# Runs of 60 KiB instead of 64 KiB in a streaming loss kernel, and three last chunks instead of two

## The chip, the cores and the metric

The kernel runs on one core of a Trainium2 chip; the other cores are idle. The metric is the device time of one execution in microseconds (us).

HBM is the chip's main memory and SBUF the core's own. 16 DMA engines move data between the two in packets; in the big transfers of this kernel one packet is the run of one partition (7680 packets of 64 KiB for 60 transfers of 128 partitions). VectorE and ScalarE compute; GpSimd issues most of the DMAs, which stand in its queue until the engines take them.

## The reference, cut to what matters

```python
pred   : (8192, 8192) float32 in 0.01 .. 0.99
target : (8192, 8192) float32, 0 or 1
pred = clip(pred, 1e-7, 1 - 1e-7)
out  = -(target * log(pred) + (1 - target) * log(1 - pred))
```

As the target is 0 or 1, the result is -log|pred + target - 1|. Three arrays of 268.44 MB cross the memory interface: two in, one out. Nothing is reused.

## The kernel before

The data is seen as 128 partitions by 524288 columns, cut into chunks. A chunk is one contiguous region of HBM, and each partition takes one contiguous run of it, so the row pitch in HBM equals the run: 16384 columns of float32 are 64 KiB. Two rings in SBUF (buffers that are filled round and round) hold two chunks: the pred in float32, overwritten in place by the result, and the target, which the DMA casts to bfloat16.

```python
RING = 32768
BIG = 16384

def plan(total):
    head = [(8192, [4096, 4096]), (8192, [8192])]
    tail = [(8192, [4096, 4096]), (8192, [4096, 2048, 2048])]
    n = (total - sum(w for w, _ in head + tail)) // BIG
    chunks = head + [(BIG, [BIG // 2] * 2)] * n + tail
    ...
def dram(flat, k):
    part = flat[cols[k] * P : (cols[k] + widths[k]) * P]
    return part.rearrange("(p w) -> p w", p=P)

def load(k):
    queue = nc.sync if k == 0 else nc.gpsimd
    nc.gpsimd.dma_start(out=span(ring_t, ...), in_=dram(target_f, k))
    queue.dma_start(out=span(ring_p, ...), in_=dram(pred_f, k))

def front(col, w):     # VectorE: clip; pred + (target - 1).  ScalarE: Abs, Ln
    ...
def back(col, w):      # VectorE: times -1
    ...
# ... (cut) per chunk: front of both pieces, back of both, store, then the loads that fit;
# in the last two chunks each piece is stored on the sync queue as soon as it is ready
```

## Time and profile before

| what | before |
|---|---|
| time, median of 3 runs | 1866.57 us (1865.54 to 1866.64) |
| span of the profiled run | 1864.5 us |
| VectorE, ScalarE busy | 60%, 48% |
| DMA row | full in all 40 slices |
| read and written in HBM | 536.87 MB, 268.44 MB |
| common packet of 64 KiB | 2418 ns |

The DMA row tells how much of the time the 16 engines had a packet in hand. It doesn't tell whether a packet was slow; for that one needs the packet durations, which are in the trace's records. A chain of waits, in contrast, has to go through something at every moment; here it goes through compute and "issue" for most of the span (ScalarE 24%, VectorE 15%, issue 25%), although the transfers beside them have no gap.

### The profile page before, as it was taken

The page shows a single profiled execution, that of the slowest core. Times are in us where ns is not written, and L with a number is a line of the kernel's source. Part 1 is how long each engine was busy: PE and PEld are TensorE (multiplying, and loading weights), DVE is VectorE, ACT ScalarE, POOL GpSimd, SP SyncE. Part 2 cuts the span into 40 slices and gives each one's busy share as a digit, 9 for nine tenths or more (in the row PEclk, how much of TensorE's full clock was granted, in tenths as well). Part 3 has the DMA queues.
Part 4 walks back from the last instruction along what each step waited for, and adds up shares of the span by engine and source line. Part 5 has one row for each costly group of instructions (what it writes and reads, how often), then busy time and mean ns, then how long its engine had stood idle before and what let it go on. Part 6 is the DMA issues. An engine that isn't in the chain of part 4 may idle for free.

```text
span 1864.5 us, 601 instructions
## 1 busy us (share of the span) xinstructions
DVE 1121.4 (60%) x205; ACT 899.3 (48%) x138; POOL 58.4 (3%) x103
## 2 busy tenths in 40 slices
DVE  4557654576545765557655576655766556665576
ACT  3366433664346643366433664335653356533566
POOL 1000000000000000000000000000000000000000
DMA  9999999999999999999999999999999999999999
GB/s 303 358 352 337 351 399 370 340 349 344 396 372 349 340 345 401 378 339 350 344 390 378 356 339 340 396 388 340 342 352 380 389 356 339 340 385 393 347 337 394
DMA packets 15124, 671.13 MB, mean 360 GB/s; under 512 B 1680, under 2 KB 1680, under 8 KB 1680
## 3 DMA queue, kind: packets, MB, share of 16 engines
q0 software_dynamic: 14256, 658.51, 98.5%
q1 hardware_dynamic: 864, 12.58, 1.6%
q14 instruction: 4, 0.03, 0.0%
HBM read 536.87 MB, written 268.44 MB: 432 GB/s over the span
## 4 chain that ended last, share of the span: by engine, by line
DMA 33%; issue 25%; ACT 24%; DVE 15%; POOL 1%; POOLq 0%; DVEq 0%; PEldq 0%
DMA ring_p<-in_pred_dram 31%; ACT ring_p L93 12%; ACT ring_p L92 12%; DVE ring_p L89 8%; DVE ring_p L86 4%; DVE ring_p L97 4%; DMA out_dram<-ring_p 1%; DMA ring_t<-in_target_dram 1%; POOL out_dram L80 1%; POOL ring_t L75 0%; POOLq L80 0%; DVEq L89 0%; PEldq L166 0%; POOLq L76 0%; POOLq L75 0%
## 5 line engine op out<-in xcount | busy, mean ns | idle before, releaser
L92 ACT ACTIVATE ring_p<-ring_p 128x8192 f32<-128x8192 f32 (+2 forms) x68 | 450.2, 6621 | 950.1 <-DVE ring_p L89 950.1
L89 DVE SCALAR_TENSOR_TENSOR ring_p<-ring_t,ring_p 128x8192 f32<-128x8192 bf16 (+2 forms) x68 | 556.9, 8190 | 2.5 <-DMA ring_t<-in_target_dram 0.2
L86 DVE TENSOR_SCALAR ring_p<-ring_p 128x8192 f32<-128x8192 f32 (+2 forms) x68 | 283.7, 4172 | 384.7 <-DMA ring_p<-in_pred_dram 384.7
L97 DVE TENSOR_SCALAR ring_p<-ring_p 128x8192 f32<-128x8192 f32 (+2 forms) x68 | 283.9, 4176 | 344.3 <-ACT ring_p L93 344.3
L93 ACT ACTIVATE ring_p<-ring_p 128x8192 f32<-128x8192 f32 (+2 forms) x68 | 450.7, 6628 | 2.2
L80 POOL DMA_DIRECT2D out_dram<-ring_p x32 | 22.3, 696 | 842.7 <-DVE ring_p L97 842.7
L76 POOL DMA_DIRECT2D ring_p<-in_pred_dram x33 | 17.7, 535 | 912.6 <-DMA out_dram<-ring_p 912.6
L75 POOL DMA_DIRECT2D ring_t<-in_target_dram x34 | 18.7, 551 | 0.8 <-PEq L166 0.8
L127 ACT ACT_TABLE_LOAD x1 | 1.3, 1283 | 0.7 <-PEq L155 0.7
L126 DVE MEMSET warm<- 1x8 f32 x1 | 0.1, 65 | 0.8 <-PEq L155 0.8
L127 ACT ACTIVATE warm<-warm 1x8 f32<-1x8 f32 x1 | 0.2, 208 | 0.0
L155 POOL MEMSET const-float32-0.0<- 128x1 f32 x1 | 0.1, 98 | 0.2 <-issue 0.2
L155 POOL MEMSET const-bfloat16-1.0<- 128x1 bf16 x1 | 0.1, 101 | 0.0
L155 POOL MEMSET const-uint8-127<- 128x1 uint8 x1 | 0.1, 99 | 0.0
L155 POOL MEMSET const-float32-1.0<- 128x1 f32 x1 | 0.1, 98 | 0.0
## 6 DMA issues: line engine op xcount, KB each, us to landing
ring_t<-in_target_dram POOLq DMA_DIRECT2D x30, 4096.0 KB, 50.0
ring_p<-in_pred_dram POOLq DMA_DIRECT2D x3, 4096.0 KB, 37.4
ring_t<-in_target_dram POOLq DMA_DIRECT2D x4, 2048.0 KB, 29.4
out_dram<-ring_p POOLq DMA_DIRECT2D x2, 4096.0 KB, 35.9
out_dram<-ring_p SPq DMA_DIRECT2D x3, 2048.0 KB, 16.2
ring_p<-in_pred_dram SPq DMA_DIRECT2D x1, 4096.0 KB, 19.7
out_dram<-ring_p SPq DMA_DIRECT2D x2, 1024.0 KB, 10.7
ring_p<-in_pred_dram POOLq DMA_DIRECT2D x30, 38.4
```

Of the source, the lines that this page charges most:

```text
L75: nc.gpsimd.dma_start(out=span(ring_t, cols[k], widths[k]), in_=dram(target_f, k))
L76: queue.dma_start(out=span(ring_p, cols[k], widths[k]), in_=dram(pred_f, k))
L80: queue.dma_start(out=dram(out_f, k)[:, off : off + w], in_=span(ring_p, cols[k] + off, w))
L86: nc.vector.tensor_scalar(out=p, in0=p, scalar1=EPS, scalar2=1 - EPS, op0=Alu.max, op1=Alu.min)
L89: nc.vector.scalar_tensor_tensor(out=p, in0=t, scalar=1.0, in1=p, op0=Alu.subtract, op1=Alu.add)
L92: nc.scalar.activation(out=p, in_=p, func=Act.Abs)
L93: nc.scalar.activation(out=p, in_=p, func=Act.Ln)
L97: nc.vector.tensor_scalar(out=p, in0=p, scalar1=-1.0, scalar2=None, op0=Alu.mult)
L126: nc.vector.memset(warm, 1.0)
L127: nc.scalar.activation(out=warm, in_=warm, func=Act.Ln)
L155: nc = _bacc.Bacc("TRN2", target_bir_lowering=False, num_devices=1)
```

## The change

Its intent: rows in HBM that lie an odd number of 4 KiB apart (15 x 4 KiB) rather than a power of two, in case such rows collide; and loads of the whole end ahead of the last big store. 15360 goes 34 times into 524288 and leaves 2048, so the end has three chunks (7680, 7680 and 2048 columns) in place of two. Its core:

```diff
-RING = 32768
-BIG = 16384
+BIG = 15 * 1024
+HALF = BIG // 2
@@ plan
-    tail = [(8192, [4096, 4096]), (8192, [4096, 2048, 2048])]
-    chunks = head + [(BIG, [BIG // 2] * 2)] * n + tail
+    spots = [(HALF, 0), (HALF, HALF)]
+    spots += [(BIG, k % 2 * BIG) for k in range(1, n - 1)]
+    end = (n - 1) % 2 * BIG
+    return spots + [(HALF, end), (HALF, end + HALF), (last, 2 * BIG)]
@@ the order is now written out ... (cut)
+        for k in range(2, n - 3):
+            front(k, (0, 2)); front(k, (1, 2)); back(k, (0, 2)); back(k, (1, 2))
+            if k < n - 4:
+                store(k)
+                for j in range(k + 2, n if k == n - 5 else k + 3):
+                    load(j)
+        store(n - 4)
+        a, b, c = n - 3, n - 2, n - 1
+        front(a)
+        front(b, (0, 2))
+        front(b, (1, 2))
+        back(a)
+        store(a)
+        front(c)
+        back(b)
+        store(b)
+        back(c)
+        store(c)
```

The last chunks are stored in pieces: two of 7680 columns and one of 2048, where there were three of 4096 and two of 2048. (The first two chunks are now computed whole.)

More of the change, by code (lines that the diff above doesn't have):

```diff
@@ L8 @@
 EPS = 1e-7
-RING = 32768
-BIG = 16384
+BIG = 15 * 1024
+HALF = BIG // 2
 def plan(total):
-    head = [(8192, [4096, 4096]), (8192, [8192])]
-    tail = [(8192, [4096, 4096]), (8192, [4096, 2048, 2048])]
-    n = (total - sum(w for w, _ in head + tail)) // BIG
-    chunks = head + [(BIG, [BIG // 2] * 2)] * n + tail
-    assert sum(w for w, _ in chunks) == total
-    return chunks, len(chunks) - len(tail)
+    n, last = divmod(total, BIG)
+    assert n > 4 and 0 < last <= 2048
+    spots = [(HALF, 0), (HALF, HALF)]
+    spots += [(BIG, k % 2 * BIG) for k in range(1, n - 1)]
+    end = (n - 1) % 2 * BIG
+    return spots + [(HALF, end), (HALF, end + HALF), (last, 2 * BIG)]
 @with_exitstack
@@ L49, with chunk, spot, store @@
     R, C = pred.shape
-    pred_f = pred.rearrange("r c -> (r c)")
-    target_f = target.rearrange("r c -> (r c)")
-    out_f = out.rearrange("r c -> (r c)")
-    total = R * C // P
+    spots = plan(R * C // P)
+    n = len(spots)
+    widths = [w for w, _ in spots]
+    cols = [sum(widths[:k]) for k in range(n)]
+    def chunk(ap, k):
+        flat = ap.rearrange("r c -> (r c)")
+        return flat[cols[k] * P : (cols[k] + widths[k]) * P].rearrange("(p w) -> p w", p=P)
     pool = ctx.enter_context(tc.tile_pool(name="rings", bufs=1))
-    ring_p = pool.tile([P, RING], fp32, name="ring_p", tag="ring_p")
-    ring_t = pool.tile([P, RING], bf16, name="ring_t", tag="ring_t")
+    ring = [P, 2 * BIG + widths[-1]]
+    ring_p = pool.tile(ring, fp32, name="ring_p", tag="ring_p")
+    ring_t = pool.tile(ring, bf16, name="ring_t", tag="ring_t")
     warm = pool.tile([1, 8], fp32, name="warm", tag="warm")
-    chunks, tail = plan(total)
-    widths = [w for w, _ in chunks]
-    cols = [sum(widths[:k]) for k in range(len(chunks))]
-    def dram(flat, k):
-        part = flat[cols[k] * P : (cols[k] + widths[k]) * P]
-        return part.rearrange("(p w) -> p w", p=P)
-    def span(ring, col, w):
-        c = col % RING
-        assert c + w <= RING
-        return ring[:, c : c + w]
+    def spot(ring, k, part=(0, 1)):
+        w, c = spots[k]
+        i, m = part
+        return ring[:, c + i * w // m : c + (i + 1) * w // m]
     def load(k):
         queue = nc.sync if k == 0 else nc.gpsimd
-        nc.gpsimd.dma_start(out=span(ring_t, cols[k], widths[k]), in_=dram(target_f, k))
-        queue.dma_start(out=span(ring_p, cols[k], widths[k]), in_=dram(pred_f, k))
-    def store(k, off, w):
-        queue = nc.sync if k >= tail else nc.gpsimd
-        queue.dma_start(
-            out=dram(out_f, k)[:, off : off + w], in_=span(ring_p, cols[k] + off, w)
-        )
-    def front(col, w):
-        p, t = span(ring_p, col, w), span(ring_t, col, w)
+        nc.gpsimd.dma_start(out=spot(ring_t, k), in_=chunk(target, k))
+        queue.dma_start(out=spot(ring_p, k), in_=chunk(pred, k))
+    def store(k):
+        queue = nc.sync if k >= n - 3 else nc.gpsimd
+        queue.dma_start(out=chunk(out, k), in_=spot(ring_p, k))
+    def front(k, *part):
+        p, t = spot(ring_p, k, *part), spot(ring_t, k, *part)
         nc.vector.tensor_scalar(
@@ L93, in front, with back @@
         nc.scalar.activation(out=p, in_=p, func=Act.Ln)
-    def back(col, w):
-        p = span(ring_p, col, w)
+    def back(k, *part):
+        p = spot(ring_p, k, *part)
         nc.vector.tensor_scalar(out=p, in0=p, scalar1=-1.0, scalar2=None, op0=Alu.mult)
-    stored = loaded = 0
-    def load_what_fits():
-        nonlocal loaded
-        while (
-            loaded < len(chunks) and cols[loaded] + widths[loaded] <= stored + RING
-        ):
-            load(loaded)
-            loaded += 1
-    waiting = []
-    def finish_one():
-        nonlocal stored
-        k, off, w = waiting.pop(0)
-        back(cols[k] + off, w)
-        if k >= tail:
-            store(k, off, w)
-        elif off + w == widths[k]:
-            store(k, 0, widths[k])
-        else:
-            return
-        stored = cols[k] + off + w
-        load_what_fits()
     with tc.manual_schedule():
-        load_what_fits()
+        for k in range(3):
+            load(k)
         nc.vector.memset(warm, 1.0)
         nc.scalar.activation(out=warm, in_=warm, func=Act.Ln)
-        for k, (_, pieces) in enumerate(chunks):
-            off = 0
-            for w in pieces:
-                front(cols[k] + off, w)
-                waiting.append((k, off, w))
-                off += w
-                if len(waiting) > 1:
-                    finish_one()
-            while waiting and k < tail:
-                finish_one()
-        while waiting:
-            finish_one()
+        front(0)
+        front(1)
+        back(0)
+        store(0)
+        back(1)
+        store(1)
+        load(3)
+        for k in range(2, n - 3):
+            front(k, (0, 2))
+            front(k, (1, 2))
+            back(k, (0, 2))
+            back(k, (1, 2))
+            if k < n - 4:
[14 more added lines that the diff above has]
+        store(c)
 _INS = ['pred', 'target']
```

## The prediction

> **What bounds the kernel now.** I read the page of the profile first, then its waits, then the stretches of time, then the timeline of one chunk, and last the DMA packet records of the trace. The page says who is busy:
>
> ```profile
> DVE 1121.4 (60%) x205; ACT 899.3 (48%) x138; POOL 58.4 (3%) x103
> ...
> DMA  9999999999999999999999999999999999999999
> ...
> q0 software_dynamic: 14256, 658.51, 98.5%
> q1 hardware_dynamic: 864, 12.58, 1.6%
> ...
> HBM read 536.87 MB, written 268.44 MB: 432 GB/s over the span
> ```
>
> VectorE and ScalarE have room; the DMA row has no gap in any slice, and the shares of the two data queues add to 100.1% of 16 engines' span. The GB/s row of the page (337 to 401) must not be taken for idle DMA: it counts written bytes, and the target is read as 4 bytes an element and written as 2. Counted by what the engines read, a chunk of 16384 columns is 3 x 8.389 MB (target, pred, result) = 25.17 MB.
>
> The chain that ended last looks different: much of it is compute and "issue". To see whether compute delays DMA I take one chunk of the steady part from the timeline, lines left out between:
>
> ```profile
> 1696.89 0.54 POOL L80 DMA_DIRECT2D out_dram<-ring_p  x1 [25.93 <-DVE ring_p L97]
> ...
> 1708.77 4.43 DVE L86 TENSOR_SCALAR ring_p<-ring_p 128x8192 f32<-128x8192 f32 x1 [12.18 <-DMA ring_p<-in_pred_dram]
> ...
> 1728.39 0.53 POOL L76 DMA_DIRECT2D ring_p<-in_pred_dram  x1 [30.42 <-DMA out_dram<-ring_p]
> ...
> 1754.79 0.54 POOL L80 DMA_DIRECT2D out_dram<-ring_p  x1 [25.87 <-DVE ring_p L97]
> 1755.32 0.55 POOL L75 DMA_DIRECT2D ring_t<-in_target_dram  x1
> 1766.74 4.43 DVE L86 TENSOR_SCALAR ring_p<-ring_p 128x8192 f32<-128x8192 f32 x1 [12.25 <-DMA ring_p<-in_pred_dram]
> ```
>
> A pred landing releases VectorE at 1708.77, and the next at 1766.74: a period of 57.97 us. The store of the chunk before had been issued at 1696.89, 11.9 us before that landing, so it stood in the queue when the load ended. The target load is issued behind the store at once and runs while the pred load waits for the store's landing (1728.39). So the large wait
>
> ```profile
> POOL ring_p L76 <- DMA out_dram<-ring_p: 912.6, 30, 31.3
> ```
>
> costs nothing: it is GpSimd standing idle while the queue is full. 25.17 MB in 57.97 us is 434 GB/s. The stretches confirm it, and show where DMA is not full (the column before the last is its share):
>
> ```profile
> 0.00:2.00 2.00, 0.07 (x1) 1.27 (x1) 0.97 (x6) 1.00 0.61 164
> ...
> 140.00:1740.00 1600.00, 974.91 (x167) 774.28 (x111) 43.89 (x82) 1.00 1.00 361
> 1740.00:1854.00 114.00, 75.83 (x23) 67.14 (x16) 4.69 (x6) 1.00 1.00 387
> 1854.00:1859.00 5.00, 0.00 (x0) 0.00 (x0) 0.00 (x0) 1.00 1.00 423
> 1859.00:1864.50 5.50, 0.00 (x0) 0.00 (x0) 0.00 (x0) 1.00 0.28 116
> ```
>
> Only the first 2 us and the last 5.5 us have free engines. Counting packets in flight at each moment, I find 1.97 us (mean of 16 engines) idle at the start, 5.26 us at the end, and none between.
>
> **Are the packets themselves slow?** This is the question the change asks, since it alters the row pitch in HBM. Of the 7680 packets of 64 KiB, 7053 took exactly 2418 ns; the mean is 2424 ns. A pred packet of 32 KiB, in the smaller chunks, takes 1213 ns. The difference, 32768 bytes in 1205 ns, is 27.19 GB/s an engine, 435.1 GB/s for 16. Packets begin about as much before the end of their forerunner (3 to 20 ns) as the 8 ns that is left over, so there is almost no cost per packet. The time above 2418 ns, summed over all 64 KiB packets and divided by 16 engines, is 3.0 us of the whole run. That is all that a better pitch could remove from them. Bytes read by the engines are 536.87 + 268.44 = 805.31 MB; at 435.1 GB/s that is 1850.9 us. Target packets take 2432 instead of 2418 ns: 14 ns x 34 loads x 8 packets an engine = 3.8 us (a little less for the smaller chunks). 1850.9 + 3.8 + 3.0 + 1.97 + 5.26 = 1864.9 us, against a span of 1864.5. The kernel is explained to half a microsecond and has some 10 us, 0.5%, above the pure movement of bytes.
>
> **What the Trainium skill says.** (1) "DMA: Bandwidth & Descriptors", section "Where 436 GB/s comes from", gives 16 ports x 256 bits x 850 MHz = 435.2 GB/s as the ceiling. The packets here show 435.1; the trace agrees. The "~358" that the same section says binds between HBM and SBUF does not bind here, with one core running: 432 GB/s over the span. (2) The same page, "Latency and other measured facts", row "HBM row pitch at large powers of two": a pitch of 512 KiB to 8 MiB cost up to half the rate, and 4 KiB of padding brought it back. This is surely the idea of the change, but the row lists no pitch as small as 64 KiB, and this trace shows 64 KiB rows moving at the port ceiling. So I take the rule as not in force here. (3) "HBM Reference", "Specifications (TRN2)": a core alone measures about 425 GB/s, bound by its 16 DMA engines; here it is 432.
>
> **The change part by part.** *Runs of 60 KiB.* Bytes stay the same, 1850.9 us. At the same rate a packet is 8 + 61440/27.19 = 2268 ns. Loads go from 34 + 34 to 37 + 37 and stores from 37 to 37 (32 chunks of 15360, four of 7680, one of 2048). The six DMAs more bring 48 packets an engine, hidden in the overlap, 14 ns x 8 x 3 = 0.3 us of target excess, and 12 completion packets of 9 or 22 ns at most 0.2 us: +0.5 us. The 3.0 us of late packets may shrink or stay; I take -0.5.
>
> *Does compute still hide?* Before, from pred landing (1708.77) to store issue (1754.79) is 46.0 us of a period of 57.97. Durations by column from the groups by form (clip 4423 and 2287 ns for 8192 and 4096 columns, subtract 8692 and 4425, activation 7022 and 3611) give for 7680 columns 4.16, 8.16 and 6.60 us: 4.16 + 8.16 + 4 x 6.60 + 4.16 + about 0.7 of handovers = 43.6 us. The period becomes 57.97 x 15/16 = 54.3, so the slack is 10.7 us instead of 11.9. Nothing emerges.
>
> *The start.* Three loads of 30720 columns hold the queue until about 74 us. The first store, now of one piece behind the second chunk's front, is issued at about 54 us and the second at about 67 us: both before the queue empties. The first packets start as before. 0 us.
>
> *The end.* Let L be the landing of the last big pred. Then the queue holds: the big store before (18.1 us), three target and pred pairs (9.2 + 9.1, 9.2 + 9.1, 2.5 + 2.5), the last big store (18.1, issued at L + 43.6), so it has work until L + 78. First half chunk: VectorE is free at L + 43.3, its front ends L + 55.6, ScalarE L + 69, VectorE takes its last step after the two fronts of the second half chunk, store at about L + 74. Second: ScalarE ends L + 83, store L + 87.3, while the first store has run out at L + 87.0. With some 1 us from issue to first packet that is a gap of about 1.3 us. Engines now end between 1859.2 and 1863.2 us, so the slowest has some of that in hand: I count +0.5. The last store is 1 MiB, as now, so the ragged end of about 5 us stays. Moving the loads ahead of the last big store gives compute cover, but there is no hole now that it could fill.
>
> Sum: +0.5 - 0.5 + 0.5 = +0.5, and -1 for what a smoother pitch may give the ragged end: about 1866 us.
>
> **The rivals.** *The pitch matters:* if odd 4 KiB pitches spread rows better, late packets vanish. For it: 133 packets above 2450 ns, in bursts of up to some 26 once a period through the first third of the run, then seldom. Against: they sum to no more than the 3.0 us. It would make 1863. *The end improves:* if all 16 engines finished together the time would fall by up to 4 us, to about 1862. Against: the last DMA has the same shape. *The store gap grows:* if compute at the end is later than I reckon, stores of the half chunks come late by 2 to 5 us, 1869 to 1871; ScalarE is the tight engine there, with 6.6 us steps. *The odd size is worse:* 60 KiB packets could cost more than bytes over rate; 2% more on each would make 1900, but the trace scales from 16 to 32 to 64 KiB (611, 1213, 2418 ns) with no jump.
>
> **Range and chances.** Gains are capped by about 3 (late packets) + 4 (ragged end) + 1 us, losses at the end by about 5: 1861 to 1871 holds it. A 2% change is 37 us; to get faster by that the ceiling of 435 GB/s would have to break, so 1%. Slower by 37 us needs slower packets or a lost overlap in every chunk: 2%.
>
> **What would show it.** Pred and store packets of 60 KiB at about 2268 ns; DMA row full; a period of 54.3 us; store issue about 10.7 us before the next pred landing; idle engines only at the start and the last 5 us, perhaps 1 us near the end. The prediction is wrong if those packets took clearly less than 2268 ns, if DMA had holes in the middle, or if GpSimd issued a store after the next load had landed.

## The result, and the profile after

| | before | after |
|---|---|---|
| time, median of 4 runs of each | 1866.39 us (1865.54 to 1866.64) | 1867.21 us (1866.96 to 1867.38) |
| span of the profiled run | 1864.5 us | 1865.4 us |

The ratio is 1.0005, with a 95% interval of 0.9988 to 1.0022: the same. The measured 1867.21 lies in the range of 1861 to 1871, 1.2 us above the point.

The page of the kernel after answers the lines shown of before; the order of the columns is the same.

```profile
DVE 1122.2 (60%) x210; ACT 899.9 (48%) x142; POOL 60.9 (3%) x111
...
q0 software_dynamic: 15408, 658.25, 98.4%
q1 hardware_dynamic: 576, 12.85, 1.7%
...
HBM read 536.87 MB, written 268.44 MB: 432 GB/s over the span
```

More packets (15408 for 14256 on the main queue), the same bytes, the same 432 GB/s, and the same share of the engines' time, 100.1% together. One chunk of the steady part, from the timeline after, lines left out between (start, duration, instruction, idle time before it and what ended it):

```profile
1699.90 0.54 POOL L78 DMA_DIRECT2D out_dram<-ring_p  x1 [24.30 <-DVE ring_p L93]
...
1711.03 4.16 DVE L82 TENSOR_SCALAR ring_p<-ring_p 128x7680 f32<-128x7680 f32 x1 [11.43 <-DMA ring_p<-in_pred_dram]
...
1754.27 0.54 POOL L78 DMA_DIRECT2D out_dram<-ring_p  x1 [24.33 <-DVE ring_p L93]
...
1765.38 4.16 DVE L82 TENSOR_SCALAR ring_p<-ring_p 128x7680 f32<-128x7680 f32 x1 [11.40 <-DMA ring_p<-in_pred_dram]
```

From one landing to the next 54.35 us (predicted 54.3); the store goes out 11.1 us before the landing (predicted 10.7). This lead is called slack below. The packet records complete the picture: of 8192 packets of 60 KiB, 7600 took exactly 2267 ns (predicted 2268), which is the rate of the 64 KiB packets. The bulk of the run is what was foretold.

The two ends differ. Here are the last microseconds in stretches: the kernel before first, then the kernel after. The columns are the stretch, its length, the busy time of VectorE, ScalarE and GpSimd, the clock, the share of time in which DMA engines were busy, and GB/s. A packet counts wholly for the stretch in which it starts, so the shares are rough in stretches this short; the times below come from the packet records.

```profile
1847.50:1850.00 2.50, 2.13 (x2) 1.47 (x1) 0.00 (x0) 1.00 0.99 426
1850.00:1852.50 2.50, 0.09 (x1) 2.35 (x2) 0.00 (x0) 1.00 1.01 433
...
1855.00:1860.00 5.00, 0.00 (x0) 0.00 (x0) 0.00 (x0) 1.00 0.91 383
1860.00:1865.00 5.00, 0.00 (x0) 0.00 (x0) 0.00 (x0) 1.00 0.19 79
```

```profile
1847.50:1850.00 2.50, 2.50 (x1) 2.47 (x2) 0.00 (x0) 1.00 0.46 197
1850.00:1852.50 2.50, 2.50 (x2) 1.06 (x1) 0.00 (x0) 1.00 0.46 197
...
1855.00:1860.00 5.00, 0.00 (x0) 0.00 (x0) 0.00 (x0) 1.00 0.91 393
1860.00:1865.00 5.00, 0.00 (x0) 0.00 (x0) 0.00 (x0) 1.00 0.73 308
```

Before, the engines are full until 1859.2 and then fall out one after the other (the ragged end): the stretch from 1860 has a share of 0.19. After, more than half of the DMA time between 1847.5 and 1852.5 is empty, and then all engines work to the very end. This hole is the wait for the store of the second 7680 chunk: the first engine ran dry at 1848.1, the last at 1851.5. (Another 0.3 us is lost at 1838, just before the store of the first.) The chain that ended last of the kernel after shows what it waited for (start, duration, what):

```profile
1843.92 3.41 ACT ring_p L89
1847.33 0.02 issue
1847.35 4.16 DVE ring_p L93
```

The logarithm of that chunk's second half ends at 1847.33, the sign step over the whole chunk at 1851.51, and the first packet of the store starts at 1852.4. From there 9.1 us for this store and 2.5 us for the last one give 1864.0; the last packet ends at 1864.18. So the end of the kernel after hangs on compute: the last 12 us of transfers could not start before it was done. In the kernel before, the engines had packets in hand from the first 2 us to the ragged end.

An account of both spans can be made from the packet records: time of the packets per engine, minus the few ns by which packets overlap, plus the time without a packet (mean of 16 engines).

| us, mean of 16 engines | before | after |
|---|---|---|
| packets | 1866.81 | 1866.91 |
| overlap | -8.13 | -8.42 |
| idle at the start | 1.97 | 1.99 |
| idle in the hole | 0 | 3.55 |
| idle at the ragged end | 3.76 | 1.33 |
| sum (span) | 1864.4 (1864.5) | 1865.4 (1865.4) |
| in the packets: late ones of 64 or 60 KiB | 3.04 | 2.48 |

"Late" is the time above the commonest duration. The hole is the 3.2 us at 1848 to 1852.4 and the 0.3 us at 1838. The change brought a hole of 3.55 us, got 2.43 us of it back at the end, and 0.56 us of late packets.

### The profile page after: what moved, and what is told of

It is laid out like the page before. It is cut to its first block, busy times and chain, and to the rows that moved or that the text cites. A ratio compares the mean times of both kernels' runs of the same rounds, so it can differ in the third digit from the quotient of the medians. Undisturbed runs are those within 1.5% of the kernel's fastest.

```text
span 1865.4 us, 619 instructions
## 1 busy us (share of the span) xinstructions
DVE 1122.2 (60%) x210; ACT 899.9 (48%) x142; POOL 60.9 (3%) x111
## 3 DMA queue, kind: packets, MB, share of 16 engines
q0 software_dynamic: 15408, 658.25, 98.4%
## 4 chain that ended last, share of the span: by engine, by line
DMA 36%; ACT 24%; issue 23%; DVE 16%; POOL 1%; DVEq 0%; POOLq 0%; PEldq 0%
DMA ring_p<-in_pred_dram 33%; ACT ring_p L88 12%; ACT ring_p L89 12%; DVE ring_p L85 8%; DVE ring_p L82 4%; DVE ring_p L93 4%; DMA out_dram<-ring_p 3%; POOL ring_t L73 0%; POOL out_dram L78 0%; DVEq L154 0%; POOLq L78 0%; DVEq L85 0%; PEldq L154 0%; POOLq L74 0%; POOLq L73 0%
## 5 line engine op out<-in xcount | busy, mean ns | idle before, releaser
L88 ACT ACTIVATE ring_p<-ring_p 128x7680 f32<-128x7680 f32 (+1 forms) x70 | 450.6, 6437 | 948.2 <-DVE ring_p L85 948.2
L85 DVE SCALAR_TENSOR_TENSOR ring_p<-ring_t,ring_p 128x7680 f32<-128x7680 bf16 (+1 forms) x70 | 557.2, 7960 | 2.4
L82 DVE TENSOR_SCALAR ring_p<-ring_p 128x7680 f32<-128x7680 f32 (+1 forms) x70 | 284.0, 4057 | 391.0 <-DMA ring_p<-in_pred_dram 391.0
L93 DVE TENSOR_SCALAR ring_p<-ring_p 128x7680 f32<-128x7680 f32 (+1 forms) x69 | 284.0, 4117 | 336.2 <-ACT ring_p L89 336.2
L89 ACT ACTIVATE ring_p<-ring_p 128x7680 f32<-128x7680 f32 (+1 forms) x70 | 451.1, 6444 | 2.2
```

Source lines behind the costliest of these rows:

```text
L82: nc.vector.tensor_scalar(out=p, in0=p, scalar1=EPS, scalar2=1 - EPS, op0=Alu.max, op1=Alu.min)
L85: nc.vector.scalar_tensor_tensor(out=p, in0=t, scalar=1.0, in1=p, op0=Alu.subtract, op1=Alu.add)
L88: nc.scalar.activation(out=p, in_=p, func=Act.Abs)
L89: nc.scalar.activation(out=p, in_=p, func=Act.Ln)
L93: nc.vector.tensor_scalar(out=p, in0=p, scalar1=-1.0, scalar2=None, op0=Alu.mult)
```

## The experiments

My theory: bytes move at the ceiling of the engines, so the pitch of 64 or 60 KiB changes next to nothing; at the end a ragged finish was exchanged for a hole. Rivals: the odd pitch does help, and the worse end hides it; the additional DMAs cost the difference; or the difference of 0.8 us is only noise. Twelve kernels were run; all gave correct results. The first four were timed in five rounds on one chip, beside nine runs of the kernel before (median 1867.23, 1866.01 to 1867.87). The others are single runs with a profile; only differences of many microseconds are read from their times, the rest from their packets.

### The changed kernel again

No edit.

> The changed kernel once more, for comparison on one chip. Theory (movement of bytes at the port ceiling; the change only exchanged a ragged end of the DMA engines for a hole before the last stores): 0.3 to 1.3 us above the kernel before, hole of about 3 us (mean of 16 engines) some 15 us from the end, all engines ending within 0.5 us. Rival (the difference of 0.8 us was the chip or the day): 0 +- 0.3 us.

Measured: 1867.38 us (1867.06 to 1867.74), ratio 1.0002 (0.9989 to 1.0015). The time on this chip can't tell the two kernels apart: runs of the kernel before alone spread over 1.9 us. The trace repeats, though: 3.39 us of hole and 1.35 us at the end, against 3.55 and 1.33 in the first trace. The exchange is real; that it costs 0.8 us net isn't shown by these times.

### The next to last chunk stored in halves

```diff
-        back(b)
-        store(b)
+        back(b, (0, 2))
+        store(b, 0, 2)
+        back(b, (1, 2))
+        store(b, 1, 2)
```

> The changed kernel, the next to last chunk stored in two halves, each as soon as it is ready. Theory: the first half is issued at about 1844 us instead of 1852, before the queue runs dry at about 1847, so the hole of about 3 us closes; the engines then end raggedly again, within about 4 us, so of the 3 us only about 1 to 1.5 come out: about 1866 us. Rival A (the hole is on the path in full): 3 us less, about 1864. Rival B (the 0.8 us come from the six DMAs more, not from the end): no change, about 1867.

Measured: 1866.59 us (1865.90 to 1867.14), 0.8 us less than the changed kernel in the same rounds; ratio to the kernel before 0.9998 (0.9984 to 1.0012). The stretches of its profile:

```profile
1847.50:1850.00 2.50, 1.70 (x1) 2.47 (x2) 0.00 (x0) 1.00 0.92 393
1850.00:1852.50 2.50, 1.23 (x1) 0.75 (x1) 0.00 (x0) 1.00 1.02 436
...
1860.00:1865.00 5.00, 0.00 (x0) 0.00 (x0) 0.00 (x0) 1.00 0.18 74
```

The hole is gone (0.05 us in the records, at 1838) and the ragged end is back: 3.14 us idle, 0.18 in the last stretch as in the kernel before. Idle in all is 5.22 us for 6.74, so 1.5 of the 3.4 us of hole came out, and the profiled spans differ by just that (1864.0 for 1865.5). The medians show 0.8 us of it. This is what the theory said, and neither rival: not the 3 us of A, and not the unchanged time of B. It is the best of the versions by its median, but not clear of the kernel before.

### The end of the kernel before, made coarse

```diff
-    tail = [(8192, [4096, 4096]), (8192, [4096, 2048, 2048])]
+    tail = [(8192, [8192]), (8192, [8192])]
```

> The kernel before, its last two chunks of 8192 columns computed and stored in one piece each. Theory: the last store is issued about 4 us after the one before it has run out, plus 1 us to its first packet: hole of about 5 us, but the ragged end of about 2.4 us goes, as lagging engines catch up in the hole: about 2.5 us more than before, 1869. Rival A (holes cost in full): 1871 to 1872. Rival B (the end is bound by movement whatever the pieces): 1866.4.

Measured: 1872.02 us (1871.34 to 1872.99), ratio 1.0027 (1.0014 to 1.0040): 4.8 us more by the medians. There are two holes, not one:

```profile
1840.00:1845.00 5.00, 4.43 (x1) 5.00 (x2) 0.00 (x0) 1.00 0.21 92
...
1855.00:1860.00 5.00, 3.75 (x1) 0.00 (x0) 0.00 (x0) 1.00 0.25 105
```

They hold 8.1 us; the ragged end went from 3.76 to 1.30 us. Idle rose by 5.7 us, so again about 2.5 us of the holes are returned because the lagging engines catch up in them. The direction and the refund are as the theory says. The size was not: I had expected one hole of 5 us, the one before the last store, which measured 4.2, and had overlooked the one before it, of 3.9. The time lies where rival A had put it (1871 to 1872), but with 8.1 us of holes; in full they would have cost 8.1, and idle time rose by 5.7. The store of the first chunk went out at 1844.8. By then half of the engines had been dry since 1841.4 and all but one since 1842.9; the last one ran dry at 1844.4. So most of the first hole comes from engines that were ahead of the slowest. The prediction left these out as well: it reckoned the queue's end from the landing of the last pred, which is the moment of the slowest engine.

### Runs of 64 KiB in the changed kernel

```diff
-BIG = 15 * 1024
+BIG = 16 * 1024
@@ the count of chunks and the size of the rings follow ... (cut)
-    return spots + [(HALF, end), (HALF, end + HALF), (last, 2 * BIG)]
+    return spots + [(HALF, end), (HALF - 2048, end + HALF), (2048, end + BIG - 2048)]
```

> The changed kernel with runs of 64 KiB again (15 * 1024 columns become 16 * 1024; the last three chunks are then 8192, 6144 and 2048 wide). Theory (pitch of 64 or 60 KiB makes no difference): common pred and store packet 2418 ns for 65536 bytes, the same 27.1 GB/s as 2267 ns for 61440; late packets sum to 2 to 3.5 us of 16 engines; hole near the end about 1.4 us by the durations on the trace; time 1865 to 1867.5, no slower than the changed kernel. Rival (the odd pitch gives something that the worse end hides): late packets sum to clearly more, time over 1869.

Measured: 1868.45 us (1867.50 to 1869.35), 1.1 us above the changed kernel. The 64 KiB packets took 2418 ns. Late packets sum to 4.1 us, above the 2 to 3.5 that I had expected, and the hole is 4.2 us where I had reckoned 1.4 (the same error once more: the slowest engine alone was dry for 1.1 us before the store's first packet at 1846.5, the first engines since 1840.5). So this run misses both sides' numbers a little. Per packet the pitch makes no difference, but the late ones came to 3.0, 3.6 and 4.1 us in three traces with 64 KiB and to 2.5, 2.7 and 2.4 us in three with 60 KiB. About 1 us, 0.05% of the run, may belong to the pitch.

### Is there a pitch that costs? Rows 512 KiB, 2048 KiB and 2040 KiB apart

Runs and schedule stay as they are; only the place of a run in HBM changes. For 512 KiB and 2048 KiB, in the kernel before (`B` is 131072 and 524288 columns):

```diff
-        part = flat[cols[k] * P : (cols[k] + widths[k]) * P]
-        return part.rearrange("(p w) -> p w", p=P)
+        block, col = divmod(cols[k], B)
+        part = flat[block * B * P : (block + 1) * B * P]
+        return part.rearrange("(p w) -> p w", p=P)[:, col : col + widths[k]]
```

> The kernel before with the same 64 KiB runs, but each partition's runs taken from a block of its own, so that rows lie 512 KiB apart in HBM instead of 64 KiB. Theory (a row of 64 KiB is moved as one packet at the port ceiling as long as the pitch is small; large powers of two collide): common packet still 2418 ns, more late packets, 0 to 4% slower (1866 to 1940 us). Rival (pitch never matters with 64 KiB runs): 1865 to 1869.

> The same with rows 2 MiB apart. Theory (large powers of two collide): packets clearly longer than 2418 ns, 10 to 35% slower (2050 to 2500 us). Rival (pitch never matters with 64 KiB runs, as each run itself spreads over the memory): 1865 to 1870 us, packets at 2418 ns.

And for 2040 KiB in the changed kernel, where all chunks but the last one form one block of 522240 columns a partition:

```diff
+        if k < n - 1:
+            rows = flat[: cols[n - 1] * P].rearrange("(p w) -> p w", p=P)
+            return rows[:, cols[k] : cols[k] + widths[k]]
```

> The changed kernel with its 60 KiB runs, each partition's runs taken from one block of its own, so that rows lie 2040 KiB apart (510 times 4 KiB: even, but no power of two). Theory (what cost 11% at 2048 KiB is the collision of rows a large power of two apart, not the distance as such): common packet 2267 ns, late packets a few us, 1866 to 1875 us. Rival A (far rows are slow at any distance): about 2080 us, as at 2048 KiB. Rival B (only an odd number of 4 KiB spreads): clearly slow, over 1900.

Measured: 1873.82 us at 512 KiB, 2079.85 us at 2048 KiB, 1867.45 us at 2040 KiB. From the page of the run at 2048 KiB:

```profile
span 2078.1 us, 601 instructions
...
q0 software_dynamic: 14256, 658.51, 97.5%
```

The DMA share is nearly as high as before (97.5% for 98.5%): the engines were seldom idle, their packets were longer. The commonest 64 KiB packet still took 2418 ns (4620 of 7680), but 2182 were more than 2% late, by 88 us of 16 engines in all, and the packets counted as 32 KiB (mostly targets) were late by another 92 us, above their common 2432 ns; idle time grew by 18 us. So the time came as expected, but not by a longer common packet. At 512 KiB the same two sums are 6.1 and 2.7 us. At 2040 KiB the late packets came to 2.2 us, as in the changed kernel, and the time is inside the 1866 to 1875 us of the theory and far from both rivals.

So the Trainium skill's row on pitches ("DMA: Bandwidth & Descriptors", section "Latency and other measured facts") holds here in direction: rows 2 MiB apart are slow, and moving off the power of two restores the rate. (The two runs differ in the run size and the schedule too, 64 KiB and the kernel before against 60 KiB and the kernel after; 60 KiB runs at 2048 KiB were not run.) It needed no odd number of 4 KiB: 2040 KiB is 510 of them. And at the pitch that this kernel had, there was nothing to restore.

### Runs of 48 and of 52 KiB

```diff
-BIG = 15 * 1024
+BIG = 12 * 1024        (and 13 * 1024)
@@
-    assert n > 4 and 0 < last <= 2048
+    assert n > 4 and 0 < last <= 8192
```

> The changed kernel with runs of 48 KiB, 12 times 4 KiB, an even number (last chunk 8192 columns). Theory (oddness does not matter at small pitches; late packets belong to the switch between loading and storing): late packets of the big size sum to 2 to 3.5 us, about the same as in the run of 52 KiB; time 1866 to 1873, with more of it at the end as the last chunk is wide. Rival (the odd pitch is what lowers the late packets from 3 to 4 us at 64 KiB to 2.5 at 60): 3.5 us or more here, 2.7 or less at 52 KiB.

> The changed kernel with runs of 52 KiB, 13 times 4 KiB, an odd number (last chunk 5120 columns). Theory: late packets of the big size sum to 2 to 3.5 us, within 1 us of the run of 48 KiB; time 1866 to 1871. Rival (odd pitch helps): 2.7 us or less, against 3.5 or more at 48 KiB.

Measured: 1881.16 us with 48 KiB and 1867.16 us with 52 KiB. Late packets came to 5.9 us with the even multiple and 2.3 us with the odd one: these are the rival's numbers, not mine. But most of the 14 us is not that. The span of the 48 KiB run is 13.2 us above that of the changed kernel: 3.4 are late packets of 48 KiB, 7.0 more idle time, as the 8192 columns of the last chunk leave 9.4 us of holes before the last stores, and 2.8 sit in the other packets. And the runs differ in something else too: the 48 KiB kernel issues its store 8.7 us before the next landing, the 52 KiB kernel 9.4 us. In the next runs late packets grow where the slack shrinks, there together with added passes. I can't separate oddness and slack with these runs. That the oddness as such matters has the 2040 KiB run against it. What stays open is whether the 1 us in runs of 64 KiB belongs to their pitch, and no time measured here would show it.

### How much slack has compute? One, two and three more passes

```diff
         nc.vector.tensor_scalar(out=p, in0=p, scalar1=-1.0, scalar2=None, op0=Alu.mult)
+        for _ in range(N if 2 <= k < n - 4 else 0):
+            nc.vector.tensor_scalar(out=p, in0=p, scalar1=1.0, scalar2=None, op0=Alu.mult)
```

> The changed kernel with two more passes of VectorE (times 1.0) behind each last step in the big chunks but the last. Theory (DMA bound, slack of about 10 us between a store's issue and the next load's landing): the first half's 8.3 us lie beside ScalarE, the second half's 8.3 us come before the store; the store is issued about 2 us before the next landing instead of 10.6; time unchanged, 1866 to 1869. Rival (compute is part of the period, as the chain that ended last suggests): +8.3 us in each of 31 chunks, about 2120 us.

> The same with three more passes. Theory: the first half now takes 16.6 us beside ScalarE's 13.2, so landing to store issue becomes about 60 us and VectorE is busy 58 us a chunk, over the 54.3 us of DMA: the slack is used up, period 58 to 60 us, 110 to 180 us slower (1980 to 2050), with holes in DMA. Rival (slack larger than thought): unchanged.

> The changed kernel with one more pass of VectorE behind each last step in the big chunks but the last; two more had cost 17 us, nearly all in late packets, three 176 us. Theory (late packets grow when the store is issued only just before the load ends): store issued about 6.5 us before the next landing, nearly all of the cost gone, 1866 to 1871. Rival (each VectorE pass disturbs the DMA by itself): half of the 17 us, 1875 to 1877.

| passes added | time (single run) | above the kernel before of the same call | VectorE busy | store ahead of next landing, median | late packets of 60 KiB |
|---|---|---|---|---|---|
| none (the first trace) | 1867.21 (median) | +0.8 | 60% | 11.1 us | 2.5 us |
| 1 | 1879.46 | +13.6 | 74% | 7.0 us | 11.9 us |
| 2 | 1884.74 | +17.5 | 87% | 3.3 us | 15.6 us |
| 3 | 2043.01 | +175.8 | 93% | 1.5 us (only the chunks where VectorE waited for the load) | 29.5 us |

The big picture fits: with two passes some 8.3 us more stand between a landing and the store in each of 31 chunks. If compute were in the period, as the rival had it, that would be 257 us; it was 17.5. With three, the work outgrows the transfers (one chunk then holds 57.9 us of VectorE work for 54.3 us of DMA), and DMA is idle for about 150 us in the middle. The waits of that run show the turn: VectorE now keeps the stores back, and seldom waits for a load (the columns: who waited for whom, us in total, times, longest).

```profile
POOL out_dram L78 <- DVE ring_p L95: 1138.3, 31, 40.0
...
DVE ring_p L82 <- DMA ring_p<-in_pred_dram: 68.2, 19, 18.8
```

But "hidden" was not quite free, and there I was wrong twice. I expected two passes to cost nothing and one to cost next to nothing. Nearly all of their cost sits in packets that took longer, while the DMA row stays full. With one pass, between 700 and 1300 us, 138 of the 145 packets that are more than 2% late start 10 to 14 us or 46 to 54 us after a pred landing, about when the engines switch from storing to loading or back. In the kernel after there is only the second group: 47 of 50 start 48 to 52 us after a landing. Both the smaller slack and the passes themselves could be the cause of the first group. The run of 48 KiB has one too, without any pass: 70 packets, 2.1 us, 4 to 7 us after a landing and nearly all in the last quarter of the run; the run of 52 KiB has 3. So a pass isn't needed for it, but there the size of the runs differs as well. The single pass, at 13.6 us, fits neither expectation. This stays open.

## Why the prediction was right

The bound and the steady part were right in their mechanism. The end was not, and the point was closer than its parts. It forecast 0.5 us less than before; the medians say 0.8 us more, the profiled spans 0.95, and the times can't tell either from none.

*The bound.* The prediction read 435.1 GB/s off packet durations and concluded that no pitch could help by more than the 3.0 us of late packets. Shown: 60 KiB packets run at the same rate, late packets went from 3.04 to 2.48 us, and the same kernel with 64 KiB runs has late packets of 4.1 us. The term was taken as -0.5 us and measured -0.56; as the traces scatter (2.2 to 2.7 us with 60 KiB, 3.0 to 4.1 with 64), so close a hit is luck. Its bursts of "up to some 26" late packets are 18 at most by a recount.

*More DMAs.* Taken as +0.5 us, with no slack lost. The packet time net of overlap, which holds the late packets too, went from 1858.68 to 1858.49 us; the sum of both terms was right to about 0.2 us. (An engine has six completion packets more, not twelve: 96 in all.)

*Compute stays hidden.* Predicted period 54.3 and slack 10.7 us; measured 54.35 and 11.1. The claim that DMA has the bulk is shown by the runs with added passes, with the reserve that the slack has a soft edge.

*The start.* Predicted no effect: 1.97 and 1.99 us idle. The first two stores were issued at 56.5 and 69.9 us, for 54 and 67, still before the queue's end at about 74.

*The end.* Two errors here partly cancel. The prediction said: "a gap of about 1.3 us", with a net +0.5, and "so the ragged end of about 5 us stays", less 1 for a smoother pitch. The gap measured 3.55 us. Its store was even early (first packet at 1852.4, which is 87.0 us after the landing at 1765.38, reckoned 88.3). The reckoned 87.0 for the queue's end fits only the slowest engine, which ran dry 86.2 us after the landing; the first was dry at 82.7. The sum had started at the landing, and that is the moment of the slowest engine. The load that landed at 1765.38 shows it: its 16 first packets (2280 ns each) start between 1742.4 and 1746.9, so eight packets later, 18.1 us, the first engine is through at 1760.5 and the last at 1765.0. And the ragged end didn't stay: it fell from 3.76 to 1.33 us, as the laggards finished in the hole, not by a smoother pitch. Net +1.1 us for a term of +0.5 - 1: this 1.6 less the 0.2 above is the miss of 1.4 us in the span. Closing the hole in one run and making holes in another show both halves of this. The loads ahead of the last big store, counted as new, were there before; they were priced at nothing.

*A wrong number.* The 5.26 us at the end were counted to 1866 us, 1.5 us past the end of the span. The right figure is 3.76, so the sum of the prediction was 1863.4 and not 1864.9, a miss of 1.1 us; that it hit the span to half a microsecond was luck. The caps on the gains, 3 + 4 + 1 us, would reach down to about 1858.5, below the stated 1861; the fastest run of any kernel took 1865.54.

*The soft side.* The prediction's cap on the gains holds: the best version tried, with the hole closed, is 0.6 us under the kernel before by its median, within the noise.

## What to carry to other kernels

When the DMA row is full, look at the packets: if most take the bytes over the rate that the bulk of them shows, and the time above that is a few us (here 3.0), spreading the rows better can gain no more than those few us, however good its reason is elsewhere. At the end of a stream, the size of the last pieces decides whether the last stores wait for compute; reckon the moment when the queue runs dry for the engine that is furthest ahead, and remember that a hole gives the lagging engines time to catch up, so part of it comes back.

## What the Trainium skill lacked or had wrong

- "DMA: Bandwidth & Descriptors", section "Latency and other measured facts", row on row pitches: it begins at 512 KiB and has copies from HBM to HBM only. Here, with loads and stores of 64 KiB runs: no loss at 64 KiB (2418 ns a packet), 0.4% at 512 KiB (1873.82 us), 11% at 2048 KiB (2079.85 us), none at 2040 KiB (1867.45 us). An odd number of 4 KiB was not needed.
- The same page, section "Where 436 GB/s comes from", says that about 358 GB/s of HBM bind for transfers between HBM and SBUF. For a core that runs alone this is too low: 432 GB/s over the whole span, 435.1 in the packets. The same page's table of measured loads and "HBM Reference" have about 425 for that case.
- "DMA: Bandwidth & Descriptors" says that engines 7 and 15 are usually slower, but no page says by how much the 16 engines of one stream drift apart: with a queue that is never empty they ended 4 us apart (3.76 us idle), after a hole within 0.2 us (1.33 us idle, nearly all of it after the last packet). The packet records don't name the engine.
- No page tells of late packets around the switches between loading and storing: 2.5 us in a run whose stores are issued 11 us before the next landing, 11.9 and 15.6 us with 7.0 and 3.3 us and more VectorE work. The cause is open.
